# A third place for the split halves of the experts' weights, and 38 tiles of scores kept on the chip where 44 were

## The chip, the cores and the metric

The kernel runs on one core of a Trainium2 chip. The time is the device time of one execution in microseconds (us), from the first to the last instruction and what lies around them. Lower is better.

## The reference, cut to what matters

One inference step of a one-layer decoder on 512 prompt tokens and 32 sample tokens (8 sequences of 4): gMLP mixing beside sparse attention, attention to a memory, then an expert layer (PEER) and a last norm. All arrays are float32. The change lies in the expert layer, which is

```
def peer_block(xb, wq, keys, u_tab, v_tab):
    T = xb.shape[0]
    q = (xb @ wq).reshape(T, PK_HEADS, 2, KEY_HALF)
    s = jnp.einsum('thcd,hcnd->thcn', q, keys, preferred_element_type=jnp.float32)
    sv, si = lax.top_k(s, PK_TOPK)
...
    fv, fi = lax.top_k(cand, PK_TOPK)
    eid = jnp.take_along_axis(cid, fi, axis=-1)
    g = jax.nn.softmax(fv, axis=-1)
    a = jax.nn.gelu(jnp.einsum('thkd,td->thk', u_tab[eid], xb))
    return jnp.einsum('thk,thkd->td', (g * a).astype(xb.dtype), v_tab[eid])
```

There are 128 x 128 = 16,384 experts with a row of 1,024 in `u_tab` and one in `v_tab`; each token takes 16 of them for each of 8 heads.

## The kernel before, in words

**Two ways to the experts.** For three of the four blocks of 128 prompt tokens (384 columns, `ND`) the kernel multiplies with all experts: the 128 tiles of `u`, each 1,024 x 128, give scores (`scores`, L1098), and the 128 tiles of `v`, each 128 x 1,024, take scores times gates to the output (`tile_out`, L1211). The first block and the samples gather the rows of their chosen experts by indirect DMA instead (`gathers`, L1721): 160 rows sets of `u` and 160 of `v`, four places (`grow`, LAG + 1), each set used by one VectorE instruction (L1744 for `u`, L1749 for `v`), after which GpSimd may issue the next gather into its place.

**Split halves.** A float32 product is made of three fast matmuls (`mm3`, L258 to L260). For that each weight tile is split (`wtile`, L227, and `split`, L219): a load from SyncE into `raw` (512 KB), a CAST on ScalarE that gives the high half `hi` (L220), and a subtract on VectorE that gives the low half `lo` (L224). L258 and L259 read `hi`, L260 reads `lo`. A tile of `u` takes 24 matmuls of 384 columns, a tile of `v` 18 of 512. `raw` has three places while the gather's pool `gp` exists: two in the pool `weights` and a third in `gp`. `hi` and `lo` have two places each, both in `weights`. The CAST of a tile writes the place of the tile two before it, so it waits until TensorE is through with that one.

**Stages.** Up to about 560 us run projections, attention and memory. The first stage of the experts (`experts`, L1122) makes the scores of 100 tiles of `u` (`AHEAD`), in the order `EARLY`. Of these, `KEEP` = 44 stay on the chip (1.5 KB per partition each); 56 go out to memory (`gd`, 192 KB each) and come back later. Beside it VectorE finds the experts of each block (`retrieve`, L972, with the maximum and index instructions of `top16`, L925 to L945) and makes gates from them (`spread`, L1048: L1075 to L1082 on VectorE, 128-column matmuls L1087 and L1088, ScalarE L1080 and L1090), which go to memory in eleven stores of 2 MB (`wd`, L1095). The gather of `u` rows runs there too. The second stage runs over the 128 tiles of `v` in order: the first 44 take kept scores, of the others 56 load theirs (L1221) and 28 (`LATE`) make them just then, with halves in a pool of their own. At tile `KEEP` the samples' routing starts. At the end come the last gathered rows, the norms (`finish`, `sample_end`) and the stores of the outputs.

**What sets the order.** Each engine runs its instructions in a fixed order that a scheduler makes when the kernel is built: it moves an instruction ahead when the places and values that it needs come free earlier by its own reckoning. So a change of the number of places changes the order on VectorE and ScalarE too. Side work (gathers, routing) is put among the tiles by `tick`, at a fixed amount for each tile.

Of the kernel before, what the change touches and what calls it, by code (L numbers as in the profile page):

```python
# [6 lines left out]
F32 = mybir.dt.float32  # L7
F32R = mybir.dt.float32r
# [10 lines left out]
P = 128  # L19
# [13 lines left out]
class Room:  # L33
    def __init__(self, ap):
        self.ap, self.at, self.slots = ap, 0, {}
# [16 lines left out]
class Kernel:  # L52
    def __init__(self, ctx, tc, I, O):
        self.ctx, self.tc, self.nc, self.I, self.O = ctx, tc, tc.nc, I, O
        self.gp, self.raws = None, -1
        self.n, self.s_routed, self.s_added = 0, False, False
        self.sides, self.chosen, self.pin, self.pin_v, self.pin_r = [], {}, None, None, None
        n, rest = P - self.AHEAD, P - self.KEEP
        self.LATE = [self.KEEP + p for p in range(rest) if (p + 1) * n // rest > p * n // rest]
        self.EARLY = [i for i in range(self.KEEP, P) if i not in self.LATE] + list(range(self.KEEP))  # L60
        self.consts()
# [164 lines left out]
    def wtile(self, pool, src, kt=KT, n=P):  # L226

        more = pool is self.pw and self.gp is not None and self.RX
        if more:
            self.raws = (self.raws + 1) % (2 + self.RX)  # L230
        raw = self.t(self.gp, [P, kt, n], tag="wraw", bufs=self.RX) if more and self.raws > 1 else self.t(pool, [P, kt, n], tag="wraw", bufs=2)
        load = self.nc.sync.dma_start(raw, src)
        self.loads += 1
        if self.todo and self.loads > 2:
            self.index_rows(load, self.nc.sync, mybir.EngineType.SP, self.PAGES)
        hi = self.t(pool, [P, kt, n], F32R, tag="whi", bufs=2)
        lo = self.t(pool, [P, kt, n], F32R, tag="wlo", bufs=2)
        self.split(hi, lo, raw)
        if self.todo and self.loads > 2:
            self.index_rows(self.pin_v, self.nc.scalar, mybir.EngineType.Activation, self.PAGES)  # L240
        return hi, lo
# [120 lines left out]
    GA = 3.0  # L362
    ORDER = "1010101R111"
    RV = True
    KEEP, MORE = 44, 19
    XB, PB, RX = 3, 3, 1
    S_AT = 0

# [753 lines left out]
    def experts(self):  # L1122
        nc, I = self.nc, self.I

        ust, kst, cst = ExitStack(), ExitStack(), ExitStack()
        self.wb = self.t(self.pool("gates", stack=ust, right=True), [P, P, 32])
        self.kept, more = {}, []
        def keep(n, name):
            pk = self.pool(name, stack=kst, right=True)
            for _ in range(n):  # L1130
                i = len(self.kept)
                self.kept[i] = self.t(pk, [P, ND])
# [746 lines left out]
```

## Time and profile before

| | us |
|---|---|
| three runs, lowest, median, highest | 1776.49, 1781.57, 1782.59 |
| the profiled execution | 1771.42 |
| its span, first to last instruction | 1769.7 |
| TensorE busy | 1647.2 |
| VectorE busy | 1476.1 |
| ScalarE busy | 863.9 |

The profiled execution is 10.15 us below the median of the three runs. Stages are told by their lines: the first CASTs of tiles of `u` fall at about 551 us, the first stage of the experts lasts to about 1107 us, where the first tile of `v` is multiplied, and the last matmul of a tile of `v` ends at 1750.5 us. PE is TensorE, PEld its weight load, DVE VectorE, ACT ScalarE, POOL GpSimd, SP SyncE. A busy TensorE says that matmuls were in flight, not that they ran at the engine's peak.

### The profile page before, as it was taken

Reading aid. Unit: us, or ns where it says so; the run is one execution under the profiler, and the core shown is the slowest. Engines: PE = TensorE matmul, PEld = TensorE weight load, DVE = VectorE, ACT = ScalarE, POOL = GpSimd, SP = SyncE. Lnnn points to the kernel's source line nnn. Section 1 sums busy time; section 2 is a strip of 40 time slices with the busy share of each in tenths; the row PEclk is TensorE's granted clock in tenths of the full one; section 3 lists DMA queues with packets and bytes.
Section 4 is the critical chain, followed back from the end, with each engine's and each line's share of the span. In section 5 each row is a group of like instructions: output and inputs, shape, how many; then the busy total and the mean of one; then the engine's idle time right before and its main releaser. Section 6 shows DMA issues by size and latency. Waiting matters only on the chain.

```text
span 1769.7 us, 29580 instructions
## 1 busy us (share of the span) xinstructions
PE 1647.2 (93%) x10238; PEld 1454.7 (82%) x10238; DVE 1476.1 (83%) x3654; ACT 863.9 (49%) x1585; POOL 499.2 (28%) x437
## 2 busy tenths in 40 slices
PE   5999879989997997999899998999999999999996
PEld 4879847879877896899889987888788888888885
DVE  4486989657669999999999975899897988878888
ACT  4246675866444336664774773333443333333333
POOL 2011024310000144232123222343333434345343
PEclk8999869999998998999999999999999999999998
DMA  6423236565754597999688779899998999999986
GB/s 210 116 77 116 79 91 209 179 211 157 229 168 137 168 360 277 328 340 335 211 297 323 268 276 298 277 346 328 374 350 303 372 358 324 354 328 326 362 304 241
DMA packets 195205, 460.33 MB, mean 260 GB/s; under 512 B 17976, under 2 KB 98616, under 8 KB 193648
## 3 DMA queue, kind: packets, MB, share of 16 engines
q1 hardware_dynamic: 127968, 239.59, 40.5%
q0 software_dynamic: 53072, 207.71, 33.1%
q10 hardware_dynamic: 14016, 11.15, 2.0%
q8 instruction: 80, 1.31, 0.3%
q14 instruction: 69, 0.57, 0.1%
HBM read 416.11 MB, written 42.05 MB: 259 GB/s over the span
## 4 chain that ended last, share of the span: by engine, by line
PE 66%; DVE 17%; DMA 6%; issue 6%; ACT 4%; POOL 1%; ACTq 0%; SPq 0%; POOLq 0%; DVEq 0%
PE t L260 20%; PE t L258 20%; PE t L259 20%; DVE t L224 3%; DMA t<-in_u,t 2%; DVE t L1744 2%; DMA t<-in_uT 1%; POOL t L1285 1%; PE t L654 1%; DMA wd<-t 1%; DVE t L942 1%; DVE t L937 1%; ACT t L220 1%; DVE t L945 1%; DVE t L933 1%
## 5 line engine op out<-in xcount | busy, mean ns | idle before, releaser
L260 PE MATMUL t<-t,t 128*128 128x384 f32 (+3 forms) x2544 | 867.6, 345 | 26.5 <-DVE t L224 26.0
L259 PE MATMUL t<-t,t 128*128 128x384 f32 (+3 forms) x2544 | 866.0, 342 | 0.0
L258 PE MATMUL t<-t,t 128*128 128x384 f32 (+3 forms) x2544 | 777.5, 345 | 12.4 <-ACT t L220 10.5
L220 ACT CAST t<-t 128x1024 fp32r<-128x1024 f32 (+4 forms) x512 | 418.5, 842 | 680.3 <-PE t L259 487.7
L224 DVE TENSOR_TENSOR t<-t,t 128x1024 fp32r<-128x1024 f32 (+4 forms) x512 | 487.5, 962 | 123.9 <-ACT t L220 120.4
L260 PEld LDWEIGHTS t<-t,t 128*128 128x128 f32 x2544 | 484.3, 191 | 76.0 <-DVE t L224 34.9
L258 PEld LDWEIGHTS t<-t,t 128*128 128x128 f32 x2544 | 484.2, 191 | 54.6 <-ACT t L220 15.3
L259 PEld LDWEIGHTS t<-t,t 128*128 128x128 f32 x2544 | 485.2, 191 | 39.9 <-issue 7.1
L1285 POOL DMA_INDIRECT t<-in_u,t x160 | 201.1, 1257 | 499.3 <-DVE t L1744 256.5
L1285 POOL DMA_INDIRECT t<-in_v,t x160 | 211.7, 1323 | 301.4 <-DVE t L1749 232.4
L1749 DVE SCALAR_TENSOR_TENSOR t<-t,t,t 128x1024 f32<-128x1024 f32 x160 | 204.7, 1279 | 3.9 <-DMA t<-in_v,t 3.0
L1744 DVE SCALAR_TENSOR_TENSOR t<-t,t 128x1024 f32<-128x1024 f32 x160 | 193.9, 1218 | 12.9 <-DMA t<-in_u,t 12.8
L1090 ACT ACTIVATE t<-t 128x512 f32<-128x512 f32 x96 | 96.9, 1147 | 28.5 <-DMA wd<-t 24.2
L1285 POOL DMA_INDIRECT t<-in_cK,t x32 | 31.4, 982 | 163.9 <-PE t L1504 86.6
L1226 DVE TENSOR_TENSOR t<-t,t 128x352 f32<-128x352 f32 x128 | 66.4, 520 | 7.2 <-DMA t<-gd 3.6
L1106 ACT ACTIVATE t<-t 128x384 f32<-128x384 f32 x128 | 62.2, 486 | 15.0 <-PE t L260 9.2
L1080 ACT ACTIVATE t<-t,t 128x128 f16<-128x128 f16 x192 | 58.8, 395 | 7.3 <-DVE t L1076 5.1
L704 ACT ACTIVATE t<-t,t 128x384 f32<-128x384 f32 x64 | 42.7, 667 | 31.8 <-DVE t L701 19.9
L1087 PE MATMUL t<-t,t 128*128 128x128 f16 x384 | 52.8, 225 | 4.8 <-DVE t L1077 2.6
L1088 PE MATMUL t<-t,t 128*128 128x128 f16 x384 | 51.2, 225 | 1.6 <-DVE t L1082 1.2
L1285 POOL DMA_INDIRECT t<-in_cV,t x32 | 34.2, 1069 | 56.2 <-PE t L1561 33.0
L1087 PEld LDWEIGHTS <-t 128*128 128x128 f16 x384 | 36.5, 100 | 12.0 <-issue 5.3
(400 smaller groups left out, 1416.6 us busy)
## 6 DMA issues: line engine op xcount, KB each, us to landing
t<-in_uT SPq DMA_DIRECT2D x128, 512.0 KB, 5.9
t<-in_v SPq DMA_DIRECT2D x128, 512.0 KB, 6.6
wd<-t POOLq DMA_DIRECT2D x11, 2048.0 KB, 9.1
t<-wd SPq DMA_DIRECT2D x32, 704.0 KB, 8.0
gd<-t SPq DMA_DIRECT2D x56, 192.0 KB, 4.4
t<-gd SPq DMA_DIRECT2D x56, 192.0 KB, 7.5
t<-in_wA SPq DMA_DIRECT2D x19, 512.0 KB, 5.6
t<-in_wO SPq DMA_DIRECT2D x16, 512.0 KB, 4.1
```

The source lines that it names most:

```text
L220: self.nc.scalar.copy(hi, x)
L224: self.pin_v = self.nc.vector.tensor_tensor(lo, x, hi, ALU.subtract)
L258: mm(out, ah, bh, start=first, stop=False)
L259: mm(out, ah, bl, start=False, stop=False)
L260: self.pin = mm(out, al, bh, start=False, stop=last)
L1087: nc.tensor.matmul(o, oj[:, x, :], oh[:, x, :], start=True, stop=False)
L1090: nc.scalar.activation(wb[:, :, t : t + 4].rearrange("p i t -> p t i"), ps.rearrange("p (t i) -> p t i", t=4), AF.Copy, scale=1.0 / 2048.0)
L1106: nc.scalar.activation(G, ps, AF.Gelu_apprx_tanh)
L1226: nc.vector.tensor_tensor(q(w)[:, : 4 * NB - 1], self.wp[:, :, i % 4, :], q(G)[:, : 4 * NB - 1], ALU.mult)
L1285: self.nc.gpsimd.indirect_dma_start(out=out, out_offset=None, in_=src, in_offset=bass.IndirectOffsetOnAxis(ap=ix, axis=0))
L1744: nc.vector.scalar_tensor_tensor(r, r, 1.0, hf, ALU.mult, ALU.mult, accum_out=a[:, k : k + 1])
L1749: nc.vector.scalar_tensor_tensor(acc, r, a[:, k : k + 1], acc, ALU.mult, ALU.add)
```

## The change

`hi` and `lo` get a third place, in a new pool `third` that is opened at the start of `experts` on the left side of memory ahead of the routing's pools; it takes 8 KB per partition. It is used whenever `raw` uses its third place, so the three go round together. The third place exists for tiles of `u` in the first stage and tiles of `v` in the second; not for the projections before, nor for the 28 tiles of `u` made in the second stage. To make room, 38 tiles of scores are kept, not 44 (9 KB per partition less): 62 go to memory and come back, the 28 late ones are spread over 90 tiles, not 84, and the samples' routing starts at tile 38.

```
-        self.gp, self.raws = None, -1
+        self.gp, self.hp, self.raws = None, None, -1
...
-        raw = self.t(self.gp, [P, kt, n], tag="wraw", bufs=self.RX) if more and self.raws > 1 else self.t(pool, [P, kt, n], tag="wraw", bufs=2)
+        def place(third, tag, dtype=F32):
+            if more and self.raws > 1 and third is not None:
+                return self.t(third, [P, kt, n], dtype, tag=tag, bufs=self.RX)
+            return self.t(pool, [P, kt, n], dtype, tag=tag, bufs=2)
+
+        raw = place(self.gp, "wraw")
...
-        hi = self.t(pool, [P, kt, n], F32R, tag="whi", bufs=2)
-        lo = self.t(pool, [P, kt, n], F32R, tag="wlo", bufs=2)
+        hi, lo = place(self.hp, "whi", F32R), place(self.hp, "wlo", F32R)
...
-    KEEP, MORE = 44, 19
+    KEEP, MORE = 38, 19
...
+        self.hp = self.pool("third", stack=ust)
```

The instructions are the same but for six more stores and six more loads of scores; the order is not. Lines after the edit carry higher numbers: by 4 up to the pool, by 5 behind it, so that L1744 of before is L1749 of after, and L1749 is L1754.

**VectorE, first stage, while the gates of the first expert block begin** (`L224 out<-raw,hi` is the subtract of a tile; the others are gates, maxima, and one gathered row). Before, the subtract ahead of these rows is that of `t_8935`, 47 printed rows up, and none stands in between:

```order
L937 MATCH_REPLACE t_8261<-t_8107,t_8082 128x128
L1075 TENSOR_TENSOR t_8580<-t_68,t_8027 128x1024
L1076 TENSOR_TENSOR t_8703<-t_68,t_8027 128x1024
L1744 SCALAR_TENSOR_TENSOR t_8612,t_7368<-t_8612,t_5107 128x1024
L224 TENSOR_TENSOR t_9000<-t_8997,t_8999 128x1024
L224 TENSOR_TENSOR t_9070<-t_9067,t_9069 128x1024
L940 MAX t_8107<-t_8255 128x8
```

So the rows of some 47 lines stand between one subtract and the next, and then two follow one another.

The same place in the changed kernel, in two pieces: first, 33 printed rows behind the subtract ahead of it,

```order
L1081 TENSOR_TENSOR t_8336<-t_8335,t_8028 128x1024
L1086 TENSOR_TENSOR t_8337<-t_8335,t_8032 128x1024
L946 MAX_INDEX t_8105<-t_8104,t_8079 128x8 x2
L224 TENSOR_TENSOR t_9181<-t_9178,t_9180 128x1024
L937 MAX t_8104<-t_8079 128x8 x3
L941 MATCH_REPLACE t_8252<-t_8104,t_8079 128x128
```

then, 31 printed rows further down:

```order
L1749 SCALAR_TENSOR_TENSOR t_8792,t_7365<-t_8792,t_5107 128x1024
L944 MAX t_8104<-t_8258 128x8
L224 TENSOR_TENSOR t_9253<-t_9250,t_9252 128x1024
L224 TENSOR_TENSOR t_9298<-t_9295,t_9297 128x1024
L224 TENSOR_TENSOR t_9335<-t_9332,t_9334 128x1024
L1081 TENSOR_TENSOR t_8701<-t_8700,t_8028 128x1024
L1080 TENSOR_TENSOR t_8817<-t_68,t_8024 128x1024
```

One subtract now stands in the middle of the long piece of other work, and three follow one another at its end, one for each place.

**VectorE, the last tile of `v`** (L1749, L1754 after: a set of gathered `v` rows is added; L1766, L1771 after: the samples' sum). Before, from the last subtract on, with six sets of rows behind it:

```order
L1749 SCALAR_TENSOR_TENSOR t_5108<-t_18890,t_7368,t_5108 128x1024
L1749 SCALAR_TENSOR_TENSOR t_5108<-t_18959,t_7368,t_5108 128x1024
L224 TENSOR_TENSOR t_19082<-t_19079,t_19081 128x1024
L1766 TENSOR_TENSOR t_97<-t_97,t_19186 128x256
L1749 SCALAR_TENSOR_TENSOR t_5108<-t_18962,t_7368,t_5108 128x1024
L1749 SCALAR_TENSOR_TENSOR t_5108<-t_18965,t_7368,t_5108 128x1024
```

and in the changed kernel, with eleven sets behind the last subtract, four of them behind L1771:

```order
L224 TENSOR_TENSOR t_19097<-t_19093,t_19096 128x384
L1754 SCALAR_TENSOR_TENSOR t_5108<-t_18833,t_7365,t_5108 128x1024
L224 TENSOR_TENSOR t_19103<-t_19100,t_19102 128x1024
L1754 SCALAR_TENSOR_TENSOR t_5108<-t_18836,t_7365,t_5108 128x1024
L1754 SCALAR_TENSOR_TENSOR t_5108<-t_18839,t_7365,t_5108 128x1024
L1754 SCALAR_TENSOR_TENSOR t_5108<-t_18875,t_7365,t_5108 128x1024
L1754 SCALAR_TENSOR_TENSOR t_5108<-t_18911,t_7365,t_5108 128x1024
L1754 SCALAR_TENSOR_TENSOR t_5108<-t_18980,t_7365,t_5108 128x1024
L1754 SCALAR_TENSOR_TENSOR t_5108<-t_18983,t_7365,t_5108 128x1024
L1754 SCALAR_TENSOR_TENSOR t_5108<-t_18986,t_7365,t_5108 128x1024
L1771 TENSOR_TENSOR t_97<-t_97,t_19207 128x256
L1754 SCALAR_TENSOR_TENSOR t_5108<-t_19022,t_7365,t_5108 128x1024
```

The last subtract stands five sets of gathered rows earlier, and the samples' sum later among them.

## Rows read from the trace of the kernel before

**Rows 1.** The page of the profiled execution: each engine's busy time, its share of the span and its instructions.

```profile
PE 1647.2 (93%) x10238; PEld 1454.7 (82%) x10238; DVE 1476.1 (83%) x3654; ACT 863.9 (49%) x1585; POOL 499.2 (28%) x437
```

**Rows 2.** Busy time by window: the first stage of the experts, the second stage up to tile 44, and from there to the last matmuls. Columns: window, length, busy us and instructions of PE, PEld, DVE, ACT, POOL, granted clock, share of the DMA engines, GB/s.

```profile
565.00:1107.00 542.00, 500.40 (x3348) 476.45 (x3347) 488.94 (x1269) 312.51 (x523) 158.82 (x132) 0.97 0.83 288
1107.00:1285.00 178.00, 175.83 (x782) 145.31 (x781) 162.90 (x238) 66.43 (x91) 67.52 (x55) 1.00 0.95 334
1285.00:1745.00 460.00, 460.00 (x2174) 398.06 (x2173) 396.65 (x618) 164.00 (x224) 191.09 (x143) 1.00 0.95 335
```

**Rows 3.** The first stage in seven windows, columns as in Rows 2.

```profile
565.00:605.00 40.00, 36.65 (x222) 35.64 (x221) 39.62 (x182) 18.21 (x25) 0.00 (x0) 0.96 0.49 156
605.00:684.00 79.00, 76.57 (x458) 74.17 (x457) 75.22 (x204) 33.87 (x56) 36.95 (x27) 1.00 0.94 331
684.00:772.00 88.00, 70.31 (x512) 64.68 (x512) 86.87 (x259) 60.49 (x106) 28.35 (x23) 0.92 0.81 295
772.00:845.00 73.00, 72.97 (x469) 71.07 (x468) 65.67 (x158) 37.69 (x61) 22.66 (x19) 1.00 0.90 325
845.00:925.00 80.00, 70.39 (x523) 66.17 (x523) 80.00 (x230) 59.42 (x103) 19.80 (x18) 0.96 0.79 266
925.00:1035.00 110.00, 109.75 (x739) 105.61 (x738) 99.27 (x176) 67.02 (x117) 34.03 (x30) 1.00 0.83 287
1035.00:1107.00 72.00, 63.75 (x436) 59.11 (x435) 42.29 (x66) 35.81 (x57) 17.03 (x15) 0.95 0.87 291
```

**Rows 4.** Who waited for whom from 565 to 1107 us: engine and line, what ended the wait, us in total, times, the longest.

```profile
ACT t L220 <- PE t L259: 163.8, 57, 13.9
...
PE t L260 <- DVE t L224: 25.4, 16, 7.9
ACT t L1090 <- DMA wd<-t: 24.2, 7, 5.2
...
PE t L258 <- ACT t L220: 8.0, 6, 2.4
```

**Rows 5.** ScalarE in order of time, where TensorE runs without a gap: start, length, instruction, and in brackets the idle time before it and what ended it.

```profile
651.01 1.06 ACT L220 CAST t<-t 128x1024 fp32r<-128x1024 f32 x1 [2.81 <-PE t L259]
...
655.17 1.05 ACT L220 CAST t<-t 128x1024 fp32r<-128x1024 f32 x1 [2.72 <-PE t L259]
```

**Rows 6.** VectorE in order of time around the first pair of subtracts of the order shown above, some of the rows.

```profile
678.63 1.21 DVE L224 TENSOR_TENSOR t<-t,t 128x1024 fp32r<-128x1024 f32 x1
...
681.05 2.41 DVE L933 MAX8 t<-t 128x8 f32<-128x128 f32 x12
...
683.70 0.28 DVE L942 FIND_INDEX8 t<-t,t 128x8 uint32<-128x128 f32 x1
...
687.65 0.67 DVE L1076 TENSOR_TENSOR t<-t,t 128x1024 f16<-128x1024 f16 x1
...
700.75 1.23 DVE L1744 SCALAR_TENSOR_TENSOR t<-t,t 128x1024 f32<-128x1024 f32 x1
...
705.03 2.36 DVE L224 TENSOR_TENSOR t<-t,t 128x1024 fp32r<-128x1024 f32 x2
```

**Rows 7.** TensorE in order of time at its longest wait in the stage (with matmuls at the lower and at the higher clock behind it), at 859 us, and at 1083 us.

```profile
706.31 0.69 PE L260 MATMUL t<-t,t 128*128 128x384 f32 x1 [7.91 <-DVE t L224]
...
707.11 0.52 PE L259 MATMUL t<-t,t 128*128 128x384 f32 x1
707.43 0.52 PE L260 MATMUL t<-t,t 128*128 128x384 f32 x1
...
710.54 0.33 PE L259 MATMUL t<-t,t 128*128 128x384 f32 x1
710.71 0.34 PE L260 MATMUL t<-t,t 128*128 128x384 f32 x1
...
859.36 0.69 PE L260 MATMUL t<-t,t 128*128 128x384 f32 x1 [4.29 <-DVE t L224]
...
1083.58 0.44 PE L258 MATMUL t<-t,t 128*128 128x384 f32 x1 [2.39 <-ACT t L220]
```

**Rows 8.** ScalarE at the wait of 1083 us.

```profile
1082.48 1.04 ACT L220 CAST t<-t 128x1024 fp32r<-128x1024 f32 x1 [5.78 <-DMA t<-in_uT]
```

**Rows 9.** The end: VectorE from the last subtract to the last gathered rows and the first output rows, then TensorE's last matmul of a tile of `v`.

```profile
1743.64 1.22 DVE L224 TENSOR_TENSOR t<-t,t 128x1024 fp32r<-128x1024 f32 x1
...
1745.10 1.28 DVE L1749 SCALAR_TENSOR_TENSOR t<-t,t,t 128x1024 f32<-128x1024 f32 x1
1746.84 1.28 DVE L1749 SCALAR_TENSOR_TENSOR t<-t,t,t 128x1024 f32<-128x1024 f32 x1 [0.46 <-DMA t<-in_v,t]
...
1754.12 1.28 DVE L1749 SCALAR_TENSOR_TENSOR t<-t,t,t 128x1024 f32<-128x1024 f32 x1 [0.64 <-DMA t<-in_v,t]
...
1759.06 2.72 DVE L1253 SCALAR_TENSOR_TENSOR t<-t,t,t 128x512 f32<-128x512 f32 x4
...
1750.13 0.39 PE L260 MATMUL t<-t,t 128*128 128x512 f32 x1
```

**Rows 10.** DMA issues, of the page: tiles of `u`, and the scores that go out and come back: count, KB each, median us from issue to landing.

```profile
t<-in_uT SPq DMA_DIRECT2D x128, 512.0 KB, 5.9
...
gd<-t SPq DMA_DIRECT2D x56, 192.0 KB, 4.4
t<-gd SPq DMA_DIRECT2D x56, 192.0 KB, 7.5
```

## The prediction

> **What bounds the kernel now.** I read the page first, then the windows by stage, then the waits of the stage where TensorE is idle, and last the engines in order of time. TensorE is busy for 93% of the span [rows 1], but not evenly. In the second stage of the experts, from 1285 to 1745 us, it is busy for 460.00 of 460 us at the full granted clock, and for 175.83 of 178 before that [rows 2]. A place more for split halves of `v` cannot shorten a stage in which no matmul waits. In the first stage it is idle for 542 - 500.40 = 41.6 us and the mean clock is 0.97 [rows 2]. That is where the change can act.
>
> The seven windows of that stage [rows 3] show two regimes. In 565 to 605, 684 to 772 and 845 to 925 us VectorE is busy for 39.62 of 40, 86.87 of 88 and 80.00 of 80 us, and TensorE is idle for 3.35, 17.69 and 9.61 us. In 772 to 845 and 925 to 1035 us TensorE is full and VectorE has 7.3 and 10.7 us to spare. In between, 605 to 684 us, both are nearly full (TensorE idle 2.43). From 1035 to 1107 us TensorE is idle for 8.25 us though VectorE has 29.7 to spare.
>
> The waits [rows 4] give the reason: of the 41.6 us, 25.4 in 16 waits end with a subtract (L224) and 8.0 with a CAST (L220). ScalarE in turn waited 163.8 us in 57 times for L259, the last reader of the place that the CAST will write. In order of time [rows 5]: 655.17 - 651.01 = 4.16 us is the pace of a tile, and before its CAST ScalarE idles 2.72 us until TensorE lets go of the place. With two places a CAST starts when the next tile starts on TensorE, so 4.16 - 1.05 (CAST) - 1.2 (subtract) = 1.9 us are left for VectorE to be late. With three it is one tile more, 6.1 us.
>
> **Part by part.** *The third place.* It removes no work. What it adds is one tile, 4.16 us, of lead that VectorE may lose before TensorE waits. Where VectorE has time to spare ahead of a full window, the lead is built up again; inside a window in which VectorE is full it can be spent once. So, window by window:
>
> - 565 to 605: the idle 3.35 us are less than one tile; all of it goes.
> - 605 to 684: 2.43 us of short waits; all of it goes.
> - 684 to 772: VectorE is full. Before, between two subtracts, it worked from 678.63 + 1.21 = 679.84 to 705.03 us, 25.2 us, on other things [rows 6], and TensorE waited 7.91 us at the end of it [rows 7]. In the changed order one subtract stands inside this piece. The first part, by its printed rows, holds 12 maxima at 0.20, 15 index and replace rows at 0.28, 5 gate rows at 0.67, 4 gathered rows at 1.23 and a small cast: 15 us. The second holds 8, 14, 8 and 4 of these and two small additions: 16 us. Together they are longer than before and TensorE has work of some 6 us for each of the two tiles, so a wait stays; only the lead of 4.16 us is saved.
> - 845 to 925: VectorE is full; the wait of 4.29 us [rows 7] and the CASTs held behind gate copies (ScalarE waits 24.2 us for the store of `wd` in the stage, at most 5.2 at a time [rows 4]) share one lead: 4.16 us of 9.61.
> - 1035 to 1107: the largest wait, 2.39 us [rows 7], follows a CAST that waited 5.78 us for its tile to land [rows 8]. The load is issued when a subtract frees its `raw` place; a subtract one tile earlier frees it 4.16 us earlier. The rest is partly gate work and the change of stages. I take half of 8.25: 4.1 us.
>
> Sum: 3.35 + 2.43 + 4.16 + 4.16 + 4.1 = 18.2 us. The bounds are nothing (the lead is never built up) and 41.6 - 4.1 = 37.5 us (every wait but half of the last window's). I take 18.2 since the rows of the full windows allow one tile each and no more.
>
> The steady idle of ScalarE, 2.7 to 2.8 us before each CAST [rows 5], is beside a TensorE that never stops there. The Trainium skill (Perfetto Trace Analysis, Optimization Strategy) says that the same gap repeating on the engine that should be saturated can mean too few buffers for the next tile. Here the repeating gap is on the engine that has time, and TensorE's gaps are irregular; read as a case of the rule all 37.5 us would go, which is the second rival below.
>
> *The clock.* Behind the wait of 7.91 us matmuls start 0.32 us apart, a little later 0.17 [rows 7]: the granted clock at its lower and its upper level (1.2 and 2.4 GHz). The means of 0.96, 0.92, 0.96 and 0.95 [rows 3] come to 1.6 + 7.0 + 3.2 + 3.6 = 15.4 us of clock not granted, part of it while TensorE was idle anyway. With the first and the 4.29 us wait gone a little returns: I take 2 us, bounds 0 and 8.
>
> *Six more tiles out and back.* Twelve transfers of 192 KB [rows 10] are 2.36 MB, 7.0 us of all DMA engines at the 335 GB/s of the second stage [rows 2], half of it in each stage. In the first the share is 0.83. In the second it is 0.95, but TensorE waits for nothing there, so I put it at nothing; without that cover it costs 3.5 us. The scores themselves are made either way. On SyncE the six stores and six loads stand in the one queue with the weight loads, whose third `raw` place already lets them run a tile ahead.
>
> *The end.* Before, the last subtract starts at 1743.64, the last matmul of `v` ends at 1750.5, and six gathered sets follow the subtract, from 1745.10 to 1754.12 us in five steps of 1.80 us, waiting for their DMA; the last is through at 1755.4 [rows 9], 4.9 us behind TensorE. Now eleven follow. The last subtract can come a tile of `v` (18 matmuls, 4.1 us) earlier, so its end is 1750.5 - 1744.9 + 4.1 = 9.7 us ahead of TensorE's; ten steps of 1.80 and 1.3 us for the last put the sets 9.6 us behind it. That is 4.7 us later, of which 1759.06 - 1755.4 = 3.7 were spent on the root of the norm before the first output row [rows 9], and still will be, beside the sets. The rest, and what the first block's own norm adds, I put at 2 us; bounds 0 and 9 (five steps with nothing beside them).
>
> Other waits: the third place's memory belonged to attention before and is read no more when the stage starts, so no wait is put down for it; starting the samples' routing six tiles earlier moves work inside a stage where TensorE is full.
>
> Sum: -18.2 - 2 + 2 = -18 us. The profiled execution took 1771.4 us, so 1753.4; on the scale of the median, 1781.6, which lies 10.2 higher, 1763.6.
>
> **The rivals.** *VectorE stays the bound.* In the three full windows it has 1.5 us to spare in 208 [rows 3], and the change takes no instruction from it. If the lead is not built up before a window, or the new order spends it, only the waits beside a VectorE with time go: 2.43 + 4.1 = 6.5 us, less 2 to 9 at the end: about 1770, on the median's scale 1780. The Trainium skill (Perfetto Trace Analysis, Identifying the Most-Contended Engine) would have the engine with the highest occupancy improved first; in those windows this is VectorE at 99%, and the trace agrees with that much. Against it: between those windows VectorE idles 7.3 and 10.7 us. A small part of this case is that the change does not do what it says, since a CAST can run ahead only if its load has landed, 5.9 us from issue [rows 10]; three subtracts in a row in the order speak against that.
>
> *All goes.* The order moves subtracts so far ahead that VectorE's side work slides into the windows where it has time: 37.5 us, with 5 of clock and 2 lost at the end, 1731, on the median's scale 1741. The second piece of 16 us in the order speaks against it.
>
> *Slower by the end.* The sets of gathered rows behind the last subtract are the mechanism: nothing else runs beside them but the norms, each step is 1.80 us, and five more are 9 us. If the first stage gives back less than 4 us, the kernel is slower by more than 5: 1771.4 - 3 + 9 = 1777.4, on the median's scale 1787.6. For it speaks that the order shows the eleven sets; against it, that the first stage would have to keep nearly all its waits.
>
> **How the numbers follow.** The forecast, -8 to -28 us, has 0.58, all goes 0.10, VectorE stays the bound 0.19, slower by the end 0.13. A measurement of this kernel tells about 0.3%, 5.3 us, from no change. Faster by more: 0.58 + 0.10 = 0.68; within it: 0.19; slower: 0.13. The range takes in the forecast's bounds and reaches into the neighbours on both sides: 32 us faster, 1750, to 1.4 slower, 1783. The forecast's own range is 1754 to 1774.
>
> **What would show it.** In the profile after: the idle time of TensorE in the first stage falls from 41.6 to about 23 us, the waits for L224 from 25.4 to about 12, and the stage ends near 1089 us. VectorE stays full near 684 to 772, and the longest wait of TensorE there is still several us. The CAST's idle before it falls to near nothing for a tile or more behind each loose window. The second stage stays at 638 us without a wait. The gathered sets end some 9 us behind the last matmul. The forecast is wrong if the second stage gets waits for a load, or if the first stage keeps 35 us of idle time.

## The result, and the profile after

The changed kernel takes 1767.64 us (median of ten runs, 1758.07 to 1774.57) beside 1779.41 for the one before on the same chip: a ratio of 0.9932, 95% interval 0.9915 to 0.9948, so 12 us faster. Run once more beside later experiments it took 1761.28 us, a ratio of 0.9916 (0.9890 to 0.9942). The forecast was 18 us.

The profiled execution took 1758.07 us with a span of 1756.3, the fastest of its ten. The executions of one program differ by some 8 us around the median, and one profile is one of them; so the changed kernel was profiled twice. Read by its marks (first matmul of `u`, first of `v`, last of `v`, end of the span), in us:

| kernel | first `u` | first `v` | last `v` | end | first stage | second | rest | TensorE idle, first stage |
|---|---|---|---|---|---|---|---|---|
| before | 560.8 | 1098.7 | 1750.1 | 1769.7 | 537.9 | 651.4 | 19.6 | 41.6 |
| changed | 562.8 | 1081.8 | 1731.6 | 1756.3 | 519.0 | 649.8 | 24.7 | 29.5 |
| changed, second profile | 564.0 | 1085.2 | 1736.1 | 1761.0 | 521.2 | 650.9 | 24.9 | 29.3 |

The first stage is 18.9 us shorter, the second 1.6, the end 5.1 longer and the start 2.0 later: -13.4 us. Before, the first tile of `v` was multiplied at 1098.7 us and not at about 1107, as the part on the profile before has it; so windows that end at 1107 before and 1092 after take in some 8 and 10 us of the second stage. The windows by stage answer to [rows 2]; columns are the window, its length, busy time of TensorE, its weight loads, VectorE, ScalarE and GpSimd, the granted clock, the DMA share and GB/s:

```profile
565.00:1092.00 527.00, 495.47 (x3345) 475.14 (x3344) 491.61 (x1282) 314.60 (x523) 160.11 (x133) 0.98 0.84 298
1092.00:1245.00 153.00, 151.48 (x679) 125.61 (x680) 138.02 (x212) 57.03 (x79) 63.30 (x48) 1.00 0.94 334
1245.00:1730.00 485.00, 485.00 (x2296) 420.97 (x2295) 415.97 (x639) 172.35 (x236) 189.57 (x148) 1.00 0.95 337
```

The seven windows of the first stage, to lay beside [rows 3]:

```profile
565.00:605.00 40.00, 39.44 (x247) 38.75 (x247) 39.32 (x178) 19.87 (x27) 0.00 (x0) 1.00 0.56 169
605.00:684.00 79.00, 79.00 (x471) 78.59 (x470) 77.61 (x205) 31.55 (x43) 32.37 (x27) 1.00 0.95 336
684.00:772.00 88.00, 78.24 (x571) 73.13 (x571) 88.00 (x247) 61.82 (x117) 28.79 (x26) 0.94 0.87 322
772.00:845.00 73.00, 67.01 (x392) 65.66 (x391) 64.78 (x153) 34.01 (x44) 28.21 (x21) 0.95 0.93 329
845.00:925.00 80.00, 79.08 (x583) 75.76 (x583) 79.76 (x222) 60.85 (x113) 21.93 (x19) 1.00 0.80 287
925.00:1035.00 110.00, 100.76 (x707) 95.85 (x705) 100.61 (x217) 69.81 (x119) 34.43 (x28) 0.97 0.79 277
1035.00:1092.00 57.00, 51.94 (x388) 47.40 (x386) 41.53 (x67) 36.70 (x63) 14.38 (x13) 1.00 0.93 314
```

In the five windows that had idle time, TensorE's idle went from 3.35, 2.43, 17.69, 9.61 and 8.25 us to 0.56, 0, 9.76, 0.92 and 5.06. In the two that had been full, 772 to 845 and 925 to 1035, there are now 5.99 and 9.24. Some 25 us went, 15 came.

What came is in TensorE's waits from 565 to 1092 us (total, times, longest), which answer to [rows 4]:

```profile
PE t L262 <- ACT t L1110: 7.8, 4, 4.2
PE t L1055 <- DVE t L1046: 7.5, 2, 6.4
PE t L264 <- DVE t L224: 6.3, 4, 4.5
PE t L262 <- ACT t L220: 3.3, 3, 1.6
PE t L1091 <- DVE t L1081: 3.1, 1, 3.1
```

The wait for a subtract (L224) fell from 25.4 to 6.3 us. New are waits for a Gelu (L1110), which frees a bank of scores (in the second profile 4.6 us, at most 1.6 at a time), and of the transposes ahead of the gates (L1055) for the index work (L1046). In order of time, all engines, at the longest of them:

```profile
978.81 1.22 DVE L224 TENSOR_TENSOR t<-t,t 128x1024 fp32r<-128x1024 f32 x1
...
982.33 1.23 DVE L224 TENSOR_TENSOR t<-t,t 128x1024 fp32r<-128x1024 f32 x1
...
982.52 0.30 PE L1055 MATMUL t<-t,t 128*128 128x128 f32 x1 [1.13 <-DVE t L1046]
983.48 1.22 DVE L1749 SCALAR_TENSOR_TENSOR t<-t,t 128x1024 f32<-128x1024 f32 x1
...
988.74 0.39 DVE L1046 TENSOR_TENSOR t<-t 128x128 f32<-128x128 f16 x1
...
989.19 0.69 PE L1055 MATMUL t<-t,t 128*128 128x128 f32 x2 [6.36 <-DVE t L1046]
989.22 1.25 ACT L1110 ACTIVATE t<-t 128x384 f32<-128x384 f32 x3 [6.92 <-DVE t L1046]
```

The reader is to see that VectorE had done the subtracts of tiles whose matmuls stand behind the transposes. It was busy all along, but with the later tile first and the index work after it. ScalarE waits for the same instruction, since the Gelu at 989.22 is the first that writes into `kept_more`, memory that the program opens only when the routing's pool `choice` closes, behind L1046. It is the only Gelu of the stage that waits for VectorE:

```profile
ACT t L1110 <- DVE t L1046: 6.9, 1, 6.9
```

Before, the last index instruction started at 969.14 us, though the tiles of `u` ran some 17 us later then:

```profile
969.14 0.41 DVE L1042 TENSOR_TENSOR t<-t 128x128 f32<-128x128 f16 x1
```

Counted in VectorE's planned order, the last block's two index results stood behind 143 and 145 subtracts of the kernel before, and stand behind 153 and 154 now. In the traces, counted from the first tile of `u`, it is 79 and 81 before, 89 and 90 now. TensorE's own order moved too, but less: it has the transposes for them behind some 76 and 78 tiles before, behind 84 now. So five and six subtracts of tiles that TensorE needs later stand ahead of the index work now, and three did before.

The end, on VectorE, answers to [rows 9]:

```profile
1721.85 1.22 DVE L224 TENSOR_TENSOR t<-t,t 128x1024 fp32r<-128x1024 f32 x1
1722.98 3.92 DVE L1754 SCALAR_TENSOR_TENSOR t<-t,t,t 128x1024 f32<-128x1024 f32 x3
...
1739.86 1.28 DVE L1754 SCALAR_TENSOR_TENSOR t<-t,t,t 128x1024 f32<-128x1024 f32 x1 [1.71 <-DMA t<-in_v,t]
...
1743.55 1.27 DVE L1754 SCALAR_TENSOR_TENSOR t<-t,t,t 128x1024 f32<-128x1024 f32 x1
```

Eleven sets in 1722.98 to 1744.82 us, ten steps of 2.06; they end 12.8 us behind the end of TensorE's last matmul of `v` (1732.0).

### The profile page after: what moved, and what is told of

The parts are those of the page before. It is cut to its first block, busy times and chain, and to the rows that moved or that the text cites. A ratio compares the mean times of both kernels' runs of the same rounds, so it can differ in the third digit from the quotient of the medians.

```text
span 1756.3 us, 29620 instructions
## 1 busy us (share of the span) xinstructions
PE 1637.6 (93%) x10237; PEld 1452.2 (83%) x10238; DVE 1474.0 (84%) x3654; ACT 865.4 (49%) x1585; POOL 496.3 (28%) x437
## 4 chain that ended last, share of the span: by engine, by line
PE 66%; DVE 16%; issue 7%; DMA 4%; ACT 3%; POOL 3%; ACTq 0%; SPq 0%; POOLq 0%; DVEq 0%
PE t L264 19%; PE t L262 19%; PE t L263 19%; DVE t L224 3%; POOL t L1290 2%; DVE t L1749 2%; PE t L658 1%; DVE t L946 1%; DMA t<-in_uT 1%; DMA t<-in_cI 1%; ACT t L220 1%; DVE t L937 1%; DMA t<-in_v,t 1%; DMA t<-x 1%; PE t L1373 1%
## 5 line engine op out<-in xcount | busy, mean ns | idle before, releaser
L263 PE MATMUL t<-t,t 128*128 128x384 f32 (+3 forms) x2544 | 866.8, 342 | 0.0
L262 PE MATMUL t<-t,t 128*128 128x384 f32 (+3 forms) x2544 | 850.7, 344 | 14.5 <-ACT t L1110 7.8
L264 PE MATMUL t<-t,t 128*128 128x384 f32 (+3 forms) x2544 | 852.9, 343 | 8.4 <-DVE t L224 8.3
L224 DVE TENSOR_TENSOR t<-t,t 128x1024 fp32r<-128x1024 f32 (+4 forms) x512 | 488.1, 964 | 127.4 <-ACT t L220 116.7
L1290 POOL DMA_INDIRECT t<-in_v,t x160 | 205.0, 1281 | 310.7 <-DVE t L1754 245.8
L1754 DVE SCALAR_TENSOR_TENSOR t<-t,t,t 128x1024 f32<-128x1024 f32 x160 | 204.8, 1280 | 6.6 <-DMA t<-in_v,t 6.1
L1749 DVE SCALAR_TENSOR_TENSOR t<-t,t 128x1024 f32<-128x1024 f32 x160 | 193.7, 1220 | 2.7 <-DMA t<-in_u,t 2.7
L1110 ACT ACTIVATE t<-t 128x384 f32<-128x384 f32 x128 | 62.4, 491 | 51.4 <-PE t L264 31.2
```

The lines of the kernel that those rows point to most:

```text
L224: self.pin_v = self.nc.vector.tensor_tensor(lo, x, hi, ALU.subtract)
L262: mm(out, ah, bh, start=first, stop=False)
L263: mm(out, ah, bl, start=False, stop=False)
L264: self.pin = mm(out, al, bh, start=False, stop=last)
L1110: nc.scalar.activation(G, ps, AF.Gelu_apprx_tanh)
L1290: self.nc.gpsimd.indirect_dma_start(out=out, out_offset=None, in_=src, in_offset=bass.IndirectOffsetOnAxis(ap=ix, axis=0))
```

## The experiments

The theory: the one tile of lead that the third place gives to both halves makes the gain, in the first stage; part of it is lost to the end and to work that the subtracts overtake. Rivals: the other number of kept tiles; a VectorE that is full in any order. Ratios are to the kernel before in the same group of runs, five rounds each.

**Kept tiles alone** (`e1_keep38_only`), from the kernel before:

```
-    KEEP, MORE = 44, 19
+    KEEP, MORE = 38, 19
```

> The kernel before with 38 tiles of scores kept in place of 44, and no third place for the halves. Theory (the third place's lead in the first stage makes the gain, the six more tiles cost nothing): first stage 538 us as before (+-3), second stage 651 (+-3), end behind the last matmul 20, time within 4 us of before. Rival (the other number of kept tiles, through the order that it makes, brings the gain): 8 to 14 us faster than before. A second rival (twelve more transfers cost on the path): 3 to 7 us slower.

1778.01 us, ratio 1.0011 (0.9996 to 1.0025). First stage 534.9, second 652.4, end 21.5 us; the wait of 7.91 us is there as before:

```profile
708.10 0.69 PE L260 MATMUL t<-t,t 128*128 128x384 f32 x1 [7.91 <-DVE t L224]
```

The number of kept tiles by itself brings none of the gain, and twelve more transfers cost nothing that can be told.

**The third place in one stage** (`e2_first_only`, `e3_second_only`), from the changed kernel; the first edit is that of the first stage alone, the other two those of the second alone:

```
-        self.pin_r = None
+        self.pin_r, self.hp = None, None
...
-        self.hp = self.pool("third", stack=ust)
+        third = self.pool("third", stack=ust)
...
-        self.pin_r = None
+        self.pin_r, self.hp = None, third
```

> The changed kernel, but the third place is used in the first stage alone; in the second the halves have two places again. The planned order then has 7 gathered sets behind the last subtract in place of 11. Theory (gain in the first stage alone, and the end longer because the third place moves the last subtracts ahead of the sets): first stage 519 us as in the changed kernel, end behind the last matmul 20 to 21 in place of 24.7, so 4 to 5 us faster than the changed kernel and some 17 faster than before. Rival (the longer end comes from the other number of kept tiles, or the second stage needs the place): end 24 to 25 us or second stage longer by 4, so no faster than the changed kernel.

> The changed kernel, but the third place is used in the second stage alone. Theory: first stage 538 us with some 40 us of idle time on TensorE, second stage 651 as it had no wait to lose, end 18 to 21 (the planned order has 5 sets behind the last subtract): within 4 us of before. Rival (part of the gain comes from the second stage or from its start): second stage shorter by 3 or more and the time 4 to 6 us under before.

First stage only: 1770.63 us, 0.9970 (0.9955 to 0.9985). Second only: 1773.66, 0.9987 (0.9973 to 1.0002). The first is faster than before, but slower than the changed kernel: the expected 4 to 5 us at the end (21.9 in place of 24.7) were there in part, and the second stage took 660.3 us in place of 649.8. TensorE's waits of this kernel from 1080 to 1305 us, and the window of the change of stages:

```profile
PE t L262 <- ACT t L220: 4.9, 4, 2.0
PE t L1192 <- DMA t<-x: 3.2, 1, 3.2
```
```profile
1087.00:1135.00 48.00, 44.13 (x216) 35.97 (x217) 31.43 (x58) 12.91 (x19) 11.06 (x9) 0.93 0.77 259
```

In the changed kernel the two waits are 1.5 and 2.2 us, and the clock over the 48 us at the change of stages is 1.00. Of the 10.5 us that the second stage takes longer here, 2.7 are idle time (6.2 in place of 3.5) and some 3.4 the clock; the rest is open. Both places together are faster than the first alone, so the second is worth something beside the first, where I saw no wait that it could remove. Alone it shows nothing: with the place in the second stage only, that stage took 653.9 us, where it took 651.4 before, and the interval of the time takes in 1. The two parts make 0.43%, both together 0.68 and 0.84%. Whether more than the sum is there, the intervals don't tell.

**The rounded half alone** (`e5_hi_only`):

```
-        hi, lo = place(self.hp, "whi", F32R), place(self.hp, "wlo", F32R)
+        hi, lo = place(self.hp, "whi", F32R), place(None, "wlo", F32R)
```

> The changed kernel with a third place for the rounded half alone; the other half, that the subtract writes, has two. Theory (TensorE waited for the subtract, and a subtract can run ahead only if its own place is free, so both halves need the third place): ScalarE's waits for L263 fall as in the changed kernel, but TensorE's waits for L224 stay at 15 to 25 us and the first stage within 5 us of before: time 0 to 5 us under before. Rival (the late CAST is what held the subtract): 8 to 14 us under before, as with both.

1778.74 us, 1.0018 (1.0001 to 1.0035): the gain is gone. TensorE's and ScalarE's waits, 565 to 1092 us:

```profile
ACT t L220 <- PE t L263: 82.7, 28, 10.1
...
PE t L262 <- ACT t L220: 12.6, 8, 3.1
...
PE t L264 <- DVE t L224: 10.8, 5, 3.4
```

The rival (8 to 14 us under before) falls. The direction is the theory's, though its 0 to 5 us under before is not there, and the size of the wait for L224 is not its either (15 to 25 expected); late CASTs took 12.6 us. But all idle time of TensorE in the first stage is 34.6 us, 7.0 less than before, and the stage, 536.4 us, is only 1.5 shorter: the same matmuls kept TensorE busy for 501.8 us in place of 496.3, at a mean granted clock of 0.96 in place of 0.97. ScalarE's wait for the readers is half of what it was [rows 4], and nothing is gained by that alone.

**The scores' stores on ScalarE** (`e4_store_act`):

```
-                    nc.sync.dma_start(self.gd[n], G)
+                    nc.scalar.dma_start(self.gd[n], G)
```

> The changed kernel, but the scores that go out are issued by ScalarE, right behind the Gelu that writes them, in place of SyncE, where a weight load stands behind each store's wait for its Gelu. Theory of what holds the rest of the idle time (loads held behind stores on SyncE: ScalarE waits 29.9 us for tiles of u, and TensorE 7.8 us for Gelus behind such CASTs): ScalarE's waits for loads fall under 12 us, TensorE's waits for Gelus to 2 or 3, first stage 513 to 516, time 3 to 6 us under the changed kernel. Rival (VectorE, full in the same windows, holds it, and the waits only change their name): first stage 519 +-2, time within 2 us of the changed kernel; the issues themselves may cost ScalarE as much.

1776.94 us, 1.0014 (0.9999 to 1.0028). ScalarE's waits for tiles of `u` fell from 29.9 to 16.8 us, but TensorE's waits grew elsewhere (565 to 1099 us):

```profile
PE t L1055 <- DVE t L1046: 11.2, 2, 7.2
PE t L1091 <- DVE t L1081: 8.3, 2, 7.0
```

Neither theory: the planned order changed with the queue, the last transposes are again behind late index work, and the first stage is 534.1 us. What the queue by itself costs stays open.

**A fourth place** (`e11_fourth`):

```
-    KEEP, MORE = 38, 19
-    XB, PB, RX = 3, 3, 1
+    KEEP, MORE = 32, 21
+    XB, PB, RX = 3, 3, 2
```

> A fourth place for raw tile and both halves, 32 tiles of scores kept in place of 38 (of these 11 from the start in place of 19). Theory of the forecast (each place gives one more tile of lead, 4.16 us, in each window in which VectorE is full): idle time in the first stage from 29 to some 18 us, time 6 to 10 us under the changed kernel. Rival (what is left are waits of other kinds, ahead of transposes and gate matmuls that TensorE has in its fixed order, and subtracts that run further ahead make them longer): idle time 27 us or more, waits for L224 next to nothing, those for index and gate work longer, time within 3 us of the changed kernel or slower.

1765.82 us, 0.9944 (0.9926 to 0.9963), beside 0.9916 for the changed kernel in the same group. Idle time 36.7 us in a first stage of 530.5, with a granted clock of 0.96. TensorE's waits, 562 to 1086 us:

```profile
PE t L1055 <- DVE t L1046: 17.9, 5, 9.4
PE t L264 <- DVE t L224: 8.9, 2, 4.7
```

The wait for the index work grew from 7.5 to 17.9 us. In the trace that work stands no further back on VectorE than in the changed kernel (behind 89 and 89 subtracts), but TensorE has the transposes behind 82 tiles, not 84: seven subtracts of later tiles now stand ahead of it, where there were five and six. The forecast's rule of a tile of gain for each place falls; the rival holds (though the waits for L224 are not next to nothing). The second stage is the shortest of all, 644.4 us.

**The changed kernel again** (`e8_after_again`) and **two places for the last 16 tiles** (`e9_last16`):

```
+        if i == P - 16:
+            self.hp = None
         vh, vl = (x.rearrange("p k d -> p (k d)") for x in self.wtile(self.pw, I["v"][i]))
```

> The changed kernel itself, once more, as the measure beside the other kernels of this group, since one profiled execution can lie several us from the median (the first one of the changed kernel was the fastest of its ten runs). Both theories: 8 to 14 us under before. Theory (third place in the first stage): idle time of TensorE in the first stage 28 to 31 us again, the wait of 6.4 us ahead of the last transposes for the gates and the 4.5 us wait near 715 us there again. Rival (the profile was a lucky one): stage time 525 us or more in this execution.

> The changed kernel, but the last 16 tiles of v get two places for their halves, so that the planned order has 8 gathered sets behind the last subtract in place of 11. Theory (the sets behind the last subtract are what made the end 5 us longer): the end behind the last matmul falls from 24.7 to 20 to 22 us, the time to 2 to 4 us under the changed kernel. Rival (the end is set by the output rows' norm and the landing of the last sets): end within 1 us of 24.7, time within 1 us of the changed kernel. A second rival (two places make TensorE wait in the last tiles): idle time of 2 us or more there.

The second profile has the same two waits (7.9 us for L1046, 4.1 at 718 us) and 29.3 us of idle time, so the first was no exception in these. With 8 sets behind the last subtract the time is 1764.57 us, 0.9936 (0.9912 to 0.9959), and the end 24.4 us in place of 24.9. VectorE there:

```profile
1743.10 1.28 DVE L1756 SCALAR_TENSOR_TENSOR t<-t,t,t 128x1024 f32<-128x1024 f32 x1
...
1748.55 1.28 DVE L1756 SCALAR_TENSOR_TENSOR t<-t,t,t 128x1024 f32<-128x1024 f32 x1 [4.10 <-DMA t<-in_v,t]
...
1749.88 1.28 DVE L1756 SCALAR_TENSOR_TENSOR t<-t,t,t 128x1024 f32<-128x1024 f32 x1
```

The last sets wait 4.10 us for their rows to land. They are through 10.6 us behind the last matmul, in place of 12.9 in the second profile of the changed kernel, but what follows them takes 13.4 us in place of 11.5. So neither the number of sets nor their landing sets the end by itself. The rival's outcome is there (end within 1 us, the times' intervals overlap); what in the norms and stores behind the sets takes the time stays open.

**The last transposes a tile later** (`e12_turn_later`), in `spread`:

```
+        if b == 2:
+            yield 50.0
...
+        with self.tc.issue_after(getattr(self.pin, "ins", self.pin)) if b == 2 else ExitStack():
+            for n, x in enumerate((i, j, g)):
+                nc.tensor.transpose(pt[:, n * P : n * P + P], x, self.ident)
```

> The changed kernel, but the last of the three sets of transposes ahead of the gates, before which TensorE waited 6.36 and 1.13 us, stands one tile of u later in TensorE's order. Theory (the subtracts that run ahead put VectorE's index work behind them, and TensorE's order did not follow): the wait there falls to 2 to 4 us, first stage 3 to 4 us shorter, time 2 to 4 us under the changed kernel. Rival (VectorE is full from 925 to 1035 us, so the wait only moves to the gate matmuls or to a subtract): idle time in the first stage within 1.5 us of the changed kernel, time the same; the gates that end a tile later may add 1 to 2 us at the change of stages.

1779.65 us, 1.0022 (1.0006 to 1.0037). TensorE at the place, and ScalarE:

```profile
992.25 0.69 PE L262 MATMUL t<-t,t 128*128 128x384 f32 x1 [8.40 <-ACT t L1113]
```
```profile
991.71 1.25 ACT L1113 ACTIVATE t<-t 128x384 f32<-128x384 f32 x3 [6.95 <-DVE t L1046]
```

The transposes no longer wait, and the next tile waits longer: for a Gelu into `kept_more`, held by the same index work. Two things hung on L1046, and freeing one showed the other. The gates, a tile late, cost more ahead of the change of stages, where TensorE waits 3.0 and 5.3 us for them (at 1081 and 1088 us). Idle time in the first stage is 41.0 us: neither the theory nor the rival (the same time) came out, and the kernel is 18 us slower than the changed one beside it.

**Index work first** (`e13_index_first`, `e14_index_far`, `e15_last_block`): a subtract may not overtake the routing instruction 24 (in the second kernel 4) places back. In the third kernel `RPIN` is 0 until `choose(3)` sets it to 1.

```
-    RPIN, RLAG = 0, 1
+    RPIN, RLAG = 1, 24
```

> The changed kernel, but each subtract of a split must stand behind the routing instruction 24 places back in the program, so that VectorE's index work for the last block stands behind 141 and 144 subtracts as in the kernel before (143 and 145) and no more behind 153 and 154; the third place stays. Theory (subtracts that may run ahead push the index work nine tiles back, and the transposes and the Gelus into the last kept tiles, whose memory the choice pool holds until then, wait for it): the waits at 976 to 995 us, 7.5 us on TensorE and 6.9 on ScalarE, are gone, idle time in the first stage 18 to 24 us in place of 29, time 4 to 9 us under the changed kernel. Rival (VectorE is full and any order only moves the wait): waits for L224 back to 15 us or more, idle time 28 or more, time within 3 us of the changed kernel or slower.

> As the kernel with 24, but with 4: the index work of the last block stands behind 132 and 133 subtracts, eleven tiles ahead of where the kernel before had it, and the last gate matmuls 15 tiles ahead of the changed kernel's. Theory (the third place's lead is spent where a long piece of routing stands between two subtracts, so that too early is bad as too late): waits for L224 of 10 to 20 us in the first stage, idle time 26 to 36 us, time 0 to 8 us over the kernel with 24. Rival (index work can't stand too early, VectorE has the time): no slower than the kernel with 24.

> The changed kernel, with the rule that a subtract stands behind the routing instruction 24 places back only from the last block's routing on: index work of the first two blocks as in the changed kernel (behind 76, 79, 90 and 93 subtracts), of the third behind 115 and of the last behind 141 and 144 in place of 118, 122, 153 and 154. Theory (in the kernel with the rule everywhere the loss of 20 us lay between 650 and 700 us, where the first gates were pulled ahead, while the waits at 976 to 995 us were gone): the first stage up to 720 us as in the changed kernel, no wait over 2 us for L1046 behind it, idle time in the first stage 18 to 25 us, time 3 to 8 us under the changed kernel, 1753 to 1758. Rival (VectorE is full and index work pulled ahead makes a subtract or a gate late elsewhere): new waits of 5 us or more ahead of gate matmuls or subtracts between 800 and 970 us, idle time 28 or more, time no better than the changed kernel.

1775.33 us, 1.0006 (0.9988 to 1.0024); 1817.99, 1.0238 (1.0212 to 1.0263); 1778.46, 0.9996 (0.9981 to 1.0011). In the first, two windows:

```profile
605.00:684.00 79.00, 62.87 (x367) 60.43 (x366) 71.57 (x215) 32.18 (x55) 34.49 (x26) 0.87 0.82 292
...
925.00:1035.00 110.00, 108.42 (x753) 103.18 (x752) 94.33 (x163) 70.98 (x121) 33.49 (x28) 1.00 0.84 296
```

The late waits are gone as the theory has it (idle 1.6 us from 925 to 1035, not 9.2), and 16 us of idle time stand at 605 to 684 us, where there was none. There, engines wait for one another in turn, as in these waits from 605 to 684 us:

```profile
PE t L1091 <- DVE t L1081: 6.8, 1, 6.8
...
PE t L1055 <- DVE t L1046: 5.3, 1, 5.3
...
DVE t L1080 <- ACT t L1084: 4.2, 2, 2.5
```

In the kernel with the rule from the last block's routing on, 20 us stand at 772 to 845 us, and the late waits are gone as well:

```profile
772.00:845.00 73.00, 52.88 (x338) 48.77 (x335) 62.36 (x202) 36.70 (x57) 15.02 (x12) 0.78 0.58 216
```
```profile
PE t L1091 <- DVE t L1081: 8.1, 3, 4.4
PE t L1055 <- DVE t L1046: 7.1, 2, 3.7
```

So the rivals' outcome (no gain, waits ahead of gates), but not by their reason: in both windows VectorE is not full, 71.57 of 79 and 62.36 of 73 us, and the waits for L224, which the first kernel's rival had back at 15 us or more, are 7.2 there. Nor did the third kernel move the last block's work alone: as its expectation says, the third block's index work moved ahead too, behind 115 subtracts in place of 118 and 122, and the waits at 816 and 821 us are those for it. So that the last block's index work by itself cannot come earlier at a gain is not shown. With 4 places back the waits for L224 are 21.9 us, nearly those of the kernel before, with three places. That kernel is 43 us slower than the one with 24, where 0 to 8 were expected: its first stage took 560.4 us with 54.9 of idle time, its second 663.0, and it started 6 us later. What made it so stays open.

## Why the prediction was right, and where it was off

- **Which stage, which wait.** Right. The first stage alone is 18.9 us shorter, more than the 13.4 net; the waits for L224 went from 25.4 to 6.3 us (12 were forecast), ScalarE's for the readers from 163.8 to 65.6, and with the place for one half, or with another number of kept tiles alone, nothing is gained.
- **18.2 us of idle time.** Measured 12.1 (41.6 to 29.5), and in the windows of [rows 3], which end 8 and 10 us later, 10.1. The two loose windows gave up 5.2 of their 5.8 us as forecast. The full windows gave more than one tile each, 7.9 and 8.7 us; the last gave 3.2. (The "some 6 us" of TensorE's work for a tile, by which a wait was to stay in the first of them, is in no row: [rows 5] has 4.16 us. A wait did stay there, of 4.5 us.) The step that failed is that the windows in which TensorE was full stay so: 15 us of new idle time stand in them. The forecast took the lead as slack that VectorE may lose. In the order it is also work that overtakes: subtracts moved ahead and index work, that transposes and the last Gelus need, went nine and ten subtracts back, while TensorE's order had it only six to eight tiles later. I had read the order where the subtracts went, at one place, and not what fell behind. That this work ends late and is waited for is shown by the rows at 989 us; that order, and not a full VectorE alone, makes it so, by the kernels with the rule, in which those waits are gone. Whether another order gives the 7 us back stays open: three kernels with another order gained nothing, but none of them moved this work on VectorE alone.
- **The clock.** 2 us forecast. The same 3,297 matmuls kept TensorE busy for 489.5 us in place of 496.3, so 6.8 of the 18.9 us are not idle time. The granted clock of the windows accounts for some 3 of them: 15.4 us not granted before, by the sum of the forecast, and 0.06 of 88, 0.05 of 73 and 0.03 of 110 us, 12.2, after. In the traces 153 matmuls of 384 columns ran at the slow pace of [rows 7] (0.24 us or more from one to the next) before and 119 do after, which makes some 5 us. So the term was mis-sized, at 3 to 7 us, within its bounds.
- **Six more tiles.** Nothing, as forecast (1.0011 with the interval at 1.0025).
- **The second stage.** Forecast: a place more cannot shorten a stage in which no matmul waits. In the two profiles it is 651.4 and 649.8, as good as said. But without the place there the kernel is slower than the changed one by 0.38% or 0.54%, so "nothing" does not hold beside the place in the first stage. Part is idle time and clock at the change of stages (2.7 and some 3.4 us in the profiles); the rest is open. One sign that the forecast named for being wrong came in small: TensorE waits 2.2 us for a load (`x`) at 1093 us, in the second stage.
- **The end.** 2 us forecast, 5.1 measured. The term was mis-sized: ten steps of 1.80 us were 2.06, and the last subtract ended 9.0 us ahead of TensorE, not 9.7, so the sets ended 12.8 us behind it and not 9.6. That their number sets the end is not so: with eight sets it is as long.
- **The start** came 2.0 us later; so it did, by 1.4, with the kept tiles alone. It was not forecast. One profile of each kernel does not tell it from chance: in the two of the changed kernel it lies 1.2 us apart.

The sum: -12.1 - 6.8 - 1.6 + 5.1 + 2.0 = -13.4 us in the first profile, beside -18. Part of that nearness is luck: idle time, end and start missed by 11.2 us to one side, clock and second stage by 6.4 to the other. "All goes" fell with the new waits; "slower by the end" had a longer end, at half its price and not shown to be by its mechanism; "VectorE stays the bound" holds in one window, 684 to 772 us, with 88.00 of 88 us and 9.76 of idle time left. The Trainium skill (Perfetto Trace Analysis, Optimization Strategy) says that the same gap repeating on the engine that should be saturated can mean too few buffers for the next tile; read as a case of it, 37.5 us would have gone with the place, and 12.1 did. The same section of the Trainium skill advises to find what blocks a gap and to make that dependency start sooner, or complete faster. The gap at 989 us names L1046, which is the first half of that advice. The kernels that started it sooner had 16 and 20 us of idle time elsewhere, but they moved other index work too, so these runs do not settle the second half.

## What to carry to other kernels

A place more lets the work that uses it overtake what stood beside it in the same engine's queue. Before counting the lead as gain, look in the new order for what falls behind and who waits for that, memory that it must free among them. Of a wait that a change brings, look for everything that hangs on the late instruction before moving one of its waiters: here there were two, and freeing one gained nothing. And do not take idle time for the whole price of waits: in the kernel with a place for one half alone 7.0 us of it went, and 5.5 came back as busy time of the same matmuls.

## What was not expected of the hardware

In the window of 772 to 845 us of the kernel with the rule in the last block, 20.1 us of idle time in waits of up to 4.4 us came with a mean clock of 0.78, 16 us of clock not granted in 73; the waits in the changed kernel, 6.0 us in that window, came with 0.95. By the trace some 10 of the 16 us fell in while matmuls were in flight. So several short waits close together took about half as much again by the clock.
